# Summing one block's expert values on VectorE, and a gate matrix laid out in 8 KB runs

## The chip, the cores and the metric

One core of a Trainium2 chip runs one program. The metric is the time of one execution on the device, in microseconds; the figure for a kernel is the median of its runs. Engines are named as the profile names them: PE is TensorE's matmul, PEld its weight load, DVE is VectorE, ACT is ScalarE, POOL is GpSimd, SP is SyncE, which issues most DMAs.

## The reference, cut to what matters

A block of a transformer: a mixer (mLSTM heads beside forgetting attention), then a channel mixer that fetches experts by product keys. Only the second is touched by the change. For each of 1024 tokens it finds 128 of 16,384 experts (8 heads, 16 each), and each expert is one row of `peer_u` and one row of `peer_v`, both 1024 floats:

```
ids  = 128 experts of each token          # from two top-16 lists per head
gate = softmax over the 16 of each head
u    = u_emb[ids]
act  = gelu(einsum('ted,td->te', u, xb))
w    = gate * act
out  = h_res + einsum('te,ted->td', w, v_emb[ids])
```

All of it is float32.

## The kernel before, in words

The 1024 tokens are four segments of two blocks of 128 tokens. The middle two segments (512 tokens) are computed **densely**: every expert is applied to every token, and a gate matrix that is zero where a token did not choose an expert picks out the right terms. The first and the last segment are computed **sparsely**: the rows of the chosen experts are gathered by indirect DMAs, 512 KB each (128 rows of 4 KB).

*Sparse part.* `gather_rows` makes the items of one block. A u item gathers the r-th expert row of each of the 128 tokens (line 326), so that token and partition agree; DVE multiplies it with the tokens and sums along the row in one instruction (line 335). A v item gathers, for one token, its 128 expert rows (line 362), so that partitions are experts, and the indices are first transposed (lines 353 to 360). Four such tokens make one step of PE: eight matmuls in the program, sixteen matmul records in the trace, which contract the 128 experts with the weights (line 384) into one accumulator `po` for the whole block. The weights `wT` are laid out by `weigh` (line 338), once per block, and a DVE copy puts four columns of them into a stationary tile of zeros before each step (line 378). At the end the residual is loaded, added and stored (lines 387 to 390). `gather_items` (line 395) gives the order in a segment: all u items of the first block (A), then four v items of A and four u items of the second block (B) in turn, and last the 128 v items of B alone.

*Gate matrix.* `gates` (line 1105) builds, for 32 tokens at a time, a tile `G` of 128 x 128 x 32 (key i, key j, token; 16 KB for each partition j), two buffers of it in turn. Each is stored to the array `gd` in memory (line 1155, 2 MB, 16 times). The last-but-one stage of the program holds this, the top-k of the last segment and some u products that are spilled for later.

*Dense stage.* It begins once `gd` is complete. The 16,384 experts are 128 tiles of 128, in 32 groups of four. For a tile `dense_u` computes the 512 tokens' products (lines 290, 1172), or loads them where they were spilled (line 1169; 12 of the 32 groups, called K below; the other 20 are R); for a group `weights` loads its gates into `Gt` (line 1220, 1 MB), DVE multiplies (line 1224), ACT and DVE split the result into a high and a low half (lines 1227, 1228); `dense_v` multiplies with the values of the group (line 1246) and DVE adds what comes out to `acc` (line 1251). Every matrix that is streamed in is split into halves likewise: ACT makes the high one (line 279), DVE the low one (line 284), with two buffers of each. The groups run K K, ten R, and then K and R in turn.

*What sets the order.* The items of the last segment are spread over the dense stage by a pacer (lines 1012 to 1049): two beats follow each product of `dense_u` (24 matmuls, or none where it is loaded) and one follows each tile of values in one half of the columns (12 matmuls), 512 beats in all, and 1.08 items are asked for in each. A gather may start when the latest dense matmul at that point of the program is done (line 1031), and its item is used `LAG = 5` steps later. There are 11 buffers for gathered rows (`GATH` 7 and `GATHV` 4). So the u items of A fall on the first 6.8 groups, the items of the second quarter and third quarter on the groups up to 21.6, and the 128 v items of B on groups 21.6 to 29. After that the dense stage runs alone. Within these bounds a planner orders every engine's instructions ahead of time, from its own estimate of durations; on the chip each engine works its list in that order.

Of the kernel before, what the change touches and what calls it, by code (L numbers as in the profile page):

```python
# [9 lines left out]
F32 = mybir.dt.float32  # L10
F32R = mybir.dt.float32r
I32 = mybir.dt.int32
U32 = mybir.dt.uint32
AF = mybir.ActivationFunctionType
OP = mybir.AluOpType
# [4 lines left out]
P = 128  # L20
D = 1024
KT = 8
# [5 lines left out]
NH_M = 4  # L28
# [17 lines left out]
DENSE = (1, 2)  # L46
NB = 2
# [3 lines left out]
GRP = 4  # L51
# [29 lines left out]
GATH = 7  # L81
GATHV = 4

JV = 14

RATE = 1.08
# [5 lines left out]
def _block_kernel(ctx, tc, nc, I, out, dbg):  # L92

    def pool(name, bufs, stack=ctx, **kw):
        return stack.enter_context(tc.tile_pool(name=name, bufs=bufs, **kw))

    cp = pool("const", 1)
    big = pool("big", 1)
    wp = pool("wp", 2)
    pp = pool("peer", 2)  # L100
    dp = pool("dram", 1, space=DRAM)
# [14 lines left out]
    st = pool("state", 1, front)  # L116
# [20 lines left out]
    dve, act, pe, pool_e, sync = nc.vector, nc.scalar, nc.tensor, nc.gpsimd, nc.sync  # L137
# [4 lines left out]
    identr = cp.tile([P, P], F32R, tag="identr", name="identr")  # L142
    dve.tensor_copy(identr, tmpi)
    ident = identr.bitcast(F32)
    negidr = cp.tile([P, P], F32R, tag="negidr", name="negidr")
    dve.tensor_scalar(negidr, tmpi, -1.0, None, op0=OP.mult)
    negid = negidr.bitcast(F32)
    tmpc = cp.tile([P, P], F32, tag="tmpc", name="tmpc")

    mask_st = cp.tile([P, P], F32R, tag="mask_st", name="mask_st")  # L150
    pool_e.memset(tmpc, 0.0)
    pool_e.affine_select(out=tmpc, in_=tmpc, compare_op=OP.is_ge, fill=-BIG, base=0,
                         pattern=[[1, P]], channel_multiplier=-1)
    dve.tensor_copy(mask_st, tmpc)

    tmpc2 = cp.tile([P, P], F32, tag="tmpc", name="tmpc2")
    mask_ts = cp.tile([P, P], F32R, tag="mask_ts", name="mask_ts")
    pool_e.memset(tmpc2, 0.0)
    pool_e.affine_select(out=tmpc2, in_=tmpc2, compare_op=OP.is_ge, fill=-BIG, base=0,
                         pattern=[[-1, P]], channel_multiplier=1)  # L160
    dve.tensor_copy(mask_ts, tmpc2)
    ones = cp.tile([P, P], F32, tag="ones", name="ones")
    pool_e.memset(ones, 1.0)
    blk2 = cp.tile([P, P], F32, tag="blk2", name="blk2")
    pool_e.memset(blk2, 0.0)
    pool_e.memset(blk2[0:64, 0:64], 1.0)
    pool_e.memset(blk2[64:128, 64:128], 1.0)
    eye4 = cp.tile([NH_M, NH_M], F32, tag="eye4", name="eye4")
    dve.tensor_copy(eye4, ident[0:NH_M, 0:NH_M])
    iota_i = cp.tile([P, P], I32, tag="tmpc", name="iota_i")  # L170
    pool_e.iota(iota_i, pattern=[[1, P]], base=0, channel_multiplier=0)
# [17 lines left out]

    Zm = []  # L190
    for i in range(2):
        z = cp.tile([P, NB, 66], F32R, tag=f"Zm{i}", name=f"Zm{i}")
        zc = cp.tile([P, 66], F32, tag="tmpc", name="zc")
        pool_e.memset(zc, 0.0)
        pool_e.memset(zc[:, 64:65], -1.0)
        dve.tensor_copy(z, zc.unsqueeze(1).broadcast_to([P, NB, 66]))
        Zm.append(z)
    gmix = cp.tile([P, KT], F32, tag="gmix", name="gmix")
    sync.dma_start(gmix, I["g_mix"])
    gbias = cp.tile([72, 1], F32, tag="gbias", name="gbias")  # L200
    sync.dma_start(gbias, I["g_bias"])
    taps = cp.tile([P, 8, 4], F32, tag="taps", name="taps")
    sync.dma_start(taps, I["taps"])
    gqk = cp.tile([P, 2], F32, tag="gqk", name="gqk")
    sync.dma_start(gqk, I["g_qk"])
    gq8 = cp.tile([P, 1], F32, tag="gq8", name="gq8")
    dve.tensor_scalar(gq8, gqk[:, 0:1], 0.125, None, op0=OP.mult)
    epsc = cp.tile([P, 1], F32, tag="epsc", name="epsc")
    pool_e.memset(epsc, EPS)

    def rsqrt(o, x, scale, t):
# [101 lines left out]
    def gather_rows(S, lb, share, room):  # L313

        b = S.xb0 + lb
        G = SimpleNamespace(S=S, lb=lb, b=b)
        G.actv = pp.tile([P, P], F32, tag="actv", name="actv")
        xn = []

        def ask(r):  # L320
            if r == 0:
                x_ = pp.tile([P, D], F32, tag="xng", name="xng", bufs=1)
                sync.dma_start(x_, xnd[b * P:(b + 1) * P, :])
                xn.append(x_)
            t = room("u", lb, r).tile([P, D], F32, tag="g", name="gu")
            d = pool_e.indirect_dma_start(out=t, out_offset=None, in_=I["peer_u"],  # L326
                                          in_offset=bass.IndirectOffsetOnAxis(ap=S.idx[:, lb, r:r + 1], axis=0))
            return t, d

        def use(r, t):  # L330
            if r % 16 in share:
                pool_e.tensor_tensor(t, t, xn[0], op=OP.mult)
                return lambda: act.activation(t, t, AF.Copy, accum_out=G.actv[:, r:r + 1])
            else:
                dve.scalar_tensor_tensor(t, t, 1.0, xn[0], op0=OP.mult, op1=OP.mult, accum_out=G.actv[:, r:r + 1])  # L335
        G.u = [(lambda r=r: ask(r), lambda t, r=r: use(r, t)) for r in range(P)]

        def weigh():
            wv = pp.tile([P, P], F32, tag="wv", name="wv", bufs=1)
            gelu = act.activation(wv, G.actv, AF.Gelu)  # L340
            with tc.issue_after(gelu.ins):
                act.preload_act_table_set(EXPLN)
            dve.tensor_mul(wv, wv, S.gate[:, lb, :])
            G.po = po_pool.tile([P, 2, 512], F32, tag="po", name="po")
            pe.transpose(G.po[:, 0, 0:P], wv, ident)
            G.wT = pp.tile([P, 4, 32], F32, tag="wT", name="wT", bufs=1)
            dve.tensor_copy(G.wT, G.po[:, 0, 0:P].rearrange("p (q j) -> p q j", q=4))

        def ask_v(tok):
            if S.idT is None:  # L350

                S.idT = []
                tp = po_pool.tile([P, 2, 512], F32, tag="po", name="idt")
                for k in range(NB):
                    idf = pp.tile([P, P], F32, tag="wv", name="idf", bufs=1)
                    dve.tensor_copy(idf, S.idx[:, k, :])
                    pe.transpose(tp[:, k, 0:P], idf, ident)
                    idT = pp.tile([P, P], I32, tag="idT", name="idT")
                    dve.tensor_copy(idT, tp[:, k, 0:P])
                    S.idT.append(idT)  # L360
            t = room("v", lb, tok % 32).tile([P, D], F32, tag="g", name="gv")
            d = pool_e.indirect_dma_start(out=t, out_offset=None, in_=I["peer_v"],  # L362
                                          in_offset=bass.IndirectOffsetOnAxis(ap=S.idT[lb][:, tok:tok + 1], axis=0))
            return t, d

        rows = {}

        def use_v(j, q, t):


            rows[q] = t
            if q < 3:
                return
            if j == 0:
                weigh()

            z = Zs[j % 2]
            dve.tensor_copy(z[:, :, 31:32], G.wT[:, :, j:j + 1])
            last = None
            with tc.high_priority():  # L380
                for n in range(2):
                    for q_ in reversed(range(4)):
                        with tc.issue_after(last.ins) if last else nullcontext():
                            last = pe.matmul(G.po[32 * q_:32 * q_ + 32, n, :], z[:, q_, 31 - j:63 - j],  # L384
                                             rows[q_][:, n * 512:(n + 1) * 512], start=(j == 0), stop=(j == 31))
            if j == 31:
                h2 = room("h", lb, j).tile([P, D], F32, tag="g", name="h2o")
                sync.dma_start(h2, h2d[b * P:(b + 1) * P, :])
                dve.tensor_add(h2, h2, G.po.rearrange("p a b -> p (a b)"))
                sync.dma_start(out[b * P:(b + 1) * P, :], h2)  # L390
        G.v = [(lambda tok=32 * q + j: ask_v(tok), lambda t, j=j, q=q: use_v(j, q, t))
               for j in range(32) for q in range(4)]
        return G

    def gather_items(S, share, room):
# [663 lines left out]
    for i in range(-1, len(SEGS)):  # L1059
# [9 lines left out]
        if i >= 0:  # L1069
            S = segs[i]  # L1070
# [28 lines left out]

    nb, xb0, nx = 2 * NB, sum(SEGS[:DENSE[0]]), DX  # L1100
    TG = 32
    gd = dp.tile([nx // TG, P, P, TG], F32, tag="gd", name="gd")
    dps = pool("dps", 2, space=PSUM)

    def gates(S, gb):

        for b in range(NB):
# [22 lines left out]
            for tg in range(P // TG):  # L1130
                G = gb.tile([P, P, TG], F32, tag="G", name="G")
                for q in range(TG // 4):
# [19 lines left out]
                    with nullcontext():  # L1152
                      act.copy(G[:, :, q * 4:q * 4 + 4].rearrange("p i t -> p t i"),  # L1153
                             bk.rearrange("p (t i) -> p t i", t=4))
                sync.dma_start(gd[(NB * (S.sg - DENSE[0]) + b) * (P // TG) + tg], G)
                yield


# [26 lines left out]
    gbs.close()  # L1185
    mid.close()
    up = pool("ahead", AHEAD + 1, reuse_waits="tile")
    rows3 = [0]

    def room3(kind, lb, i):  # L1190
# [24 lines left out]
    def weights(g):  # L1215

        res = []
        Gt = ds_.tile([P, nx // TG, GRP, TG], F32, tag="Gt", name="Gt", bufs=2)
        e0 = order[g] * GRP
        sync.dma_start(Gt, gd[:, :, e0:e0 + GRP, :].rearrange("b j i t -> j b i t"))  # L1220
        for ii in range(GRP):
            w = ws[g * GRP + ii]
            w3 = w.rearrange("p (b t) -> p b t", t=TG)
            dve.tensor_mul(w3, w3, Gt[:, :, ii, :])
            Wh = ds_.tile([P, 512], F32R, tag="Wh", name="Wh", bufs=2 * GRP)
            Wl = ds_.tile([P, 512], F32R, tag="Wl", name="Wl", bufs=2 * GRP)
            act.copy(Wh, w)  # L1227
            dve.tensor_sub(Wl, w, Wh.bitcast(F32))
            res.append((Wh, Wl))
        return res  # L1230
# [80 lines left out]
```

## Time and profile before

| | us |
|---|---|
| median of 3 runs (lowest, highest) | 3333.57 (3333.47, 3339.92) |
| the profiled execution | 3322.29 |
| its span in the profile | 3320.4 |

| engine | busy us | share of the span | instructions |
|---|---|---|---|
| PE | 3004.0 | 90% | 14225 |
| DVE | 2210.0 | 67% | 5506 |
| ACT | 1060.2 | 32% | 1961 |
| POOL | 1375.3 | 41% | 1233 |

DMA moved 931.18 MB, on average 280 GB/s. The profile is read by stage: a share over the whole span mixes stages with different limits. "Busy" of several instructions that overlap counts the stretch once in the tables of windows; the mean duration of one instruction can be longer than the distance from its start to the next one's.

### The profile page before, as it was taken

What the parts mean: (1) busy time and instruction counts of PE and PEld (TensorE: products, weight loads), DVE (VectorE), ACT (ScalarE), POOL (GpSimd) and SP (SyncE); (2) the same over time, 40 slices, a digit from 0 to 9 for tenths busy, and PEclk for the clock granted to TensorE, in tenths of its full rate; (3) what the DMA queues carried; (4) which work ended last, traced back from release to release, by engine and by line L of the source; (5) the groups of instructions that cost most, each with busy time, mean ns of one, the idle gap of its engine ahead of it and who ended that gap; (6) DMA issues with size and microseconds to landing.
All of it is one profiled execution on the core that took longest, in us unless ns stands there. A gap on an engine that the chain in (4) does not pass through costs nothing. (4 is left out here: it accounts for less than half of the span.)

```text
span 3320.4 us, 41585 instructions
## 1 busy us (share of the span) xinstructions
PE 3004.0 (90%) x14225; PEld 2196.0 (66%) x14225; DVE 2210.0 (67%) x5506; ACT 1060.2 (32%) x1961; POOL 1375.3 (41%) x1233
## 2 busy tenths in 40 slices
PE   8999789567977889999999876999999999999999
PEld 4566567444754667766468765777777777776666
DVE  3242579996546996556378996888667777674443
ACT  1323423223222322222246683222322322232221
POOL 1000055575456554445564302544435444443442
PEclk9988899878979889999999888999999999999999
DMA  4535488998999988888986637988889999998995
GB/s 136 137 109 138 152 292 276 288 317 292 342 309 360 324 286 246 253 264 312 357 307 232 257 166 263 315 305 318 291 299 366 346 357 340 336 335 317 340 339 199
DMA packets 373816, 931.18 MB, mean 280 GB/s; under 512 B 57268, under 2 KB 143508, under 8 KB 371556
## 3 DMA queue, kind: packets, MB, share of 16 engines
q0 software_dynamic: 161216, 552.56, 47.4%
q1 hardware_dynamic: 212388, 375.96, 33.5%
q8 instruction: 112, 1.84, 0.2%
q14 instruction: 100, 0.82, 0.1%
HBM read 860.91 MB, written 67.47 MB: 280 GB/s over the span
## 5 line engine op out<-in xcount | busy, mean ns | idle before, releaser
L326 POOL DMA_INDIRECT gu<-in_peer_u,idx x512 | 598.5, 1169 | 749.7 <-DVE gu L335 165.9
L362 POOL DMA_INDIRECT gv<-in_peer_v,idT x512 | 547.5, 1069 | 605.0 <-PE po L384 360.7
L335 DVE SCALAR_TENSOR_TENSOR gu<-gu,xng 128x1024 f32<-128x1024 f32 x496 | 614.7, 1255 | 95.9 <-DMA gu<-in_peer_u,idx 89.2
L279 ACT CAST wh<-raw 128x1024 fp32r<-128x1024 f32 x288 | 301.9, 1049 | 822.2 <-PE vo L1246 282.3
L284 DVE TENSOR_TENSOR wl<-raw,wh 128x1024 fp32r<-128x1024 f32 x262 | 323.3, 1234 | 283.3 <-ACT wh L279 235.8
L1246 PE MATMUL vo<-wh,Wh 128*128 128x512 f32 x1024 | 377.6, 397 | 34.7 <-ACT Wh L1227 18.2
L1246 PE MATMUL vo<-wl,Wh 128*128 128x512 f32 x1024 | 403.3, 394 | 0.0
L1246 PE MATMUL vo<-wh,Wl 128*128 128x512 f32 x1024 | 401.4, 393 | 0.0
L303 PE MATMUL fp<-hnh,raw 128*128 128x256 f32 (+1 forms) x1024 | 253.8, 406 | 36.7 <-DVE frs L630 23.1
L384 PE MATMUL po<-gv,Z 128*32 128x512 f32 x2048 | 257.9, 613 | 9.5 <-DMA gv<-in_peer_v,idT 8.4
L1246 PEld LDWEIGHTS vo<-wh,Wh 128*128 128x128 f32 x1024 | 194.6, 190 | 98.6 <-issue 23.5
L303 PEld LDWEIGHTS fp<-hnh,raw 128*128 128x128 f32 x1024 | 203.9, 203 | 78.7 <-DVE frs L630 24.7
L290 PE MATMUL du<-xh,wl 128*128 128x512 f32 x640 | 250.3, 391 | 0.0
L290 PE MATMUL du<-xl,wh 128*128 128x512 f32 x640 | 250.2, 391 | 0.0
L290 PE MATMUL du<-xh,wh 128*128 128x512 f32 x640 | 249.9, 390 | 0.0
L1246 PEld LDWEIGHTS vo<-wl,Wh 128*128 128x128 f32 x1024 | 194.1, 190 | 48.9 <-issue 8.4
L1246 PEld LDWEIGHTS vo<-wh,Wl 128*128 128x128 f32 x1024 | 193.9, 189 | 48.2 <-issue 7.5
L430 PE MATMUL tk<-raw,hnh 128*128 128x512 f32 (+1 forms) x416 | 195.3, 617 | 4.1 <-DMA raw<-in_wt 3.0
L1151 PE MATMUL gout<-A,B 128*128 128x128 f32 x1024 | 155.8, 303 | 43.2 <-DVE A L1149 16.8
L1251 DVE TENSOR_TENSOR acc<-acc,vo 128x512 f32<-128x512 f32 x256 | 167.2, 684 | 32.6 <-PE vo L1246 30.2
L1151 PEld LDWEIGHTS gout<-A,B 128*128 128x128 f32 x1024 | 141.1, 209 | 66.3 <-ACT G L1153 23.4
L1227 ACT CAST Wh<-w 128x512 fp32r<-128x512 f32 x128 | 79.4, 621 | 289.0 <-PE vo L1246 164.4
(407 smaller groups left out, 5165.4 us busy)
## 6 DMA issues: line engine op xcount, KB each, us to landing
raw<-in_ut SPq DMA_DIRECT2D x128, 512.0 KB
raw<-in_peer_v SPq DMA_DIRECT2D x128, 512.0 KB
raw<-in_wf SPq DMA_DIRECT2D x64, 512.0 KB
gd<-G SPq DMA_DIRECT2D x16, 2048.0 KB
Gt<-gd SPq DMA_DIRECT2D x32, 1024.0 KB
raw<-in_wt SPq DMA_DIRECT2D x48, 512.0 KB
raw<-in_wq SPq DMA_DIRECT2D x48, 512.0 KB
raw<-in_wo SPq DMA_DIRECT2D x32, 512.0 KB
```

Of the source, the lines that this page charges most:

```text
L279: seen["act"] = act.copy(h, raw)
L284: seen["dve"] = dve.tensor_sub(l, raw, h.bitcast(F32))
L290: seen["pe"] = pe.matmul(o, w, x[:, c], start=(first and i == 0), stop=(last and i == 2))
L303: pe.matmul(o, raw[:, k * P:(k + 1) * P], xh[:, k, c], start=(k == 0), stop=(k == KT - 1))
L326: d = pool_e.indirect_dma_start(out=t, out_offset=None, in_=I["peer_u"], in_offset=bass.IndirectOffsetOnAxis(ap=S.idx[:, lb, r:r + 1], axi ...
L335: dve.scalar_tensor_tensor(t, t, 1.0, xn[0], op0=OP.mult, op1=OP.mult, accum_out=G.actv[:, r:r + 1])
L362: d = pool_e.indirect_dma_start(out=t, out_offset=None, in_=I["peer_v"], in_offset=bass.IndirectOffsetOnAxis(ap=S.idT[lb][:, tok:tok + 1], ...
L384: last = pe.matmul(G.po[32 * q_:32 * q_ + 32, n, :], z[:, q_, 31 - j:63 - j], rows[q_][:, n * 512:(n + 1) * 512], start=(j == 0), stop=(j ...
L430: pe.matmul(b[0:w, :], xh[:, k, s0:s0 + w], raw[:, k % 2 * 512:(k % 2 + 1) * 512], start=(k == 0), stop=(k == KT - 1))
L1151: pe.matmul(bk[:, u * P:(u + 1) * P], B[:, u, :], A[:, u, :], start=True, stop=True)
L1246: seen["pe"] = pe.matmul(bks[b], w[:, cw], v, start=(ii == 0 and i == 0), stop=(ii == GRP - 1 and i == 2))
L1251: dve.tensor_add(o, o, bks[b])
```

## The change

The v items of the second block of the last segment (`VDVE`) are done as its u items are: item r gathers the r-th expert row of each of the 128 tokens, by `S.idx` itself, and DVE multiplies it with the token's weight and adds it to a sum `G.sum` of 128 x 1024 floats. Before the first of them ACT computes gelu, DVE multiplies with the gate, and the sum is loaded with the residual from `h2d`; after the last the sum is stored. The 512 matmul records of that block, its weight transpose, its 32 column copies, the final addition, one index transpose and one reload of an ACT table are no longer there.

The array `gd` is laid out as [group of four tiles][j][32-token block][4 tiles x 32 tokens] in place of [32-token block][j][i][token]. A load of `Gt` then reads 8 KB in one run for each partition, where it read 16 runs of 512 B; a store of `G` writes 32 runs of 512 B for each partition, 1 MB apart, where it wrote one of 16 KB.

Constant tiles that only the first stages use are placed in the pool `st`, whose memory is given back when these stages end. The sum tile takes 4 KB for each partition.

```diff
+VDVE = ((3, 1),)
...
-    ones = cp.tile([P, P], F32, tag="ones", name="ones")
+    ones = st.tile([P, P], F32, tag="ones", name="ones")
...
-                for k in range(NB):
+                for k in [k for k in range(NB) if (S.sg, k) not in VDVE]:
...
-        G.v = [(lambda tok=32 * q + j: ask_v(tok), lambda t, j=j, q=q: use_v(j, q, t))
-               for j in range(32) for q in range(4)]
+        def ask_r(r):
+            t = room("v", lb, r).tile([P, D], F32, tag="g", name="gr")
+            d = pool_e.indirect_dma_start(out=t, out_offset=None, in_=I["peer_v"],
+                                          in_offset=bass.IndirectOffsetOnAxis(ap=S.idx[:, lb, r:r + 1], axis=0))
+            return t, d
+
+        def use_r(r, t):
+
+            if r == 0:
+                G.wv = pp.tile([P, P], F32, tag="wr", name="wr", bufs=1)
+                gelu = act.activation(G.wv, G.actv, AF.Gelu)
+                dve.tensor_mul(G.wv, G.wv, S.gate[:, lb, :])
+                G.sum = sums.tile([P, D], F32, tag="gsum", name="gsum", bufs=1)
+                sync.dma_start(G.sum, h2d[b * P:(b + 1) * P, :])
+            dve.scalar_tensor_tensor(G.sum, t, G.wv[:, r:r + 1], G.sum, op0=OP.mult, op1=OP.add)
+            if r == P - 1:
+                sync.dma_start(out[b * P:(b + 1) * P, :], G.sum)
+        if (S.sg, lb) in VDVE:
+            G.v = [(lambda r=r: ask_r(r), lambda t, r=r: use_r(r, t)) for r in range(P)]
+        else:
+            G.v = [(lambda tok=32 * q + j: ask_v(tok), lambda t, j=j, q=q: use_v(j, q, t))
+                   for j in range(32) for q in range(4)]
...
-    gd = dp.tile([nx // TG, P, P, TG], F32, tag="gd", name="gd")
+    gd = dp.tile([P // GRP, P, nx // TG, GRP * TG], F32, tag="gd", name="gd")
...
-                sync.dma_start(gd[(NB * (S.sg - DENSE[0]) + b) * (P // TG) + tg], G)
+                sync.dma_start(gd[:, :, (NB * (S.sg - DENSE[0]) + b) * (P // TG) + tg, :].rearrange("g j c -> j g c"),
+                               G.rearrange("p (g i) t -> p g (i t)", i=GRP))
...
+    sums = pool("sums", 1, reuse_waits="tile")
...
-        e0 = order[g] * GRP
-        sync.dma_start(Gt, gd[:, :, e0:e0 + GRP, :].rearrange("b j i t -> j b i t"))
+        sync.dma_start(Gt, gd[order[g]].rearrange("j b (i t) -> j b i t", i=GRP))
```

## Rows read from the trace of the kernel before

**Rows 1.** Windows by stage: busy us by engine, granted PE clock, DMA share, GB/s.

```profile
core 0: us, PE busy (x) PEld busy (x) DVE busy (x) ACT busy (x) POOL busy (x), PEclk, DMA share, GB/s
1671.00:1925.00 254.00, 226.93 (x1306) 185.79 (x1302) 229.19 (x809) 151.42 (x278) 122.05 (x110) 0.92 0.71 264
1925.00:2007.40 82.40, 61.23 (x387) 52.30 (x387) 70.24 (x198) 76.95 (x145) 0.00 (x0) 0.94 0.35 150
2007.40:2024.20 16.80, 0.00 (x0) 0.00 (x0) 1.34 (x3) 0.61 (x1) 0.00 (x0) 0.53 1.00 353
2133.50:2319.80 186.30, 176.85 (x769) 145.06 (x769) 156.86 (x235) 51.04 (x64) 88.31 (x70) 0.99 0.89 310
2319.80:2992.00 672.20, 671.72 (x3164) 510.49 (x3165) 469.71 (x695) 195.57 (x252) 301.74 (x267) 1.00 0.93 334
2992.00:3290.00 298.00, 298.00 (x1527) 200.87 (x1526) 126.36 (x183) 75.14 (x97) 122.38 (x118) 1.00 0.89 319
3290.00:3320.40 30.40, 24.16 (x107) 19.68 (x105) 12.15 (x16) 3.15 (x3) 0.00 (x0) 0.98 0.22 87
```

**Rows 2.** Chain that ended last, 3010 to 3043 us: start, us, what.

```profile
3010.19 7.48 PE vo L1246 x32
...
3024.35 11.15 PE vo L1246 x48
3035.49 1.85 PE po L384 x16
3037.35 5.69 PE du L290 x24
```

**Rows 3.** Groups by line, 2992 to 3290 us: busy us, mean ns | idle before.

```profile
L384 PE MATMUL po<-gv,Z 128*32 128x512 f32 x512 | 62.6, 598 | 0.0
L284 DVE TENSOR_TENSOR wl<-raw,wh 128x1024 fp32r<-128x1024 f32 x43 | 52.7, 1226 | 79.8 <-ACT wh L279 50.9 <-issue 14.3 <-PE du L290 13.8
L1251 DVE TENSOR_TENSOR acc<-acc,vo 128x512 f32<-128x512 f32 x52 | 34.5, 685 | 12.6 <-PE vo L1246 11.3 <-issue 1.1
L1228 DVE TENSOR_TENSOR Wl<-w,Wh 128x512 fp32r<-128x512 f32 x27 | 18.6, 691 | 29.2 <-ACT Wh L1227 19.3 <-PE vo L1246 5.8 <-issue 4.1
L1224 DVE TENSOR_TENSOR w<-w,Gt 128x512 f32<-128x512 f32 x27 | 18.0, 685 | 2.7 <-ACT w L1173 2.7
```

**Rows 4.** Groups by line, 2133.5 to 2319.8 us, four R groups with u items.

```profile
L335 DVE SCALAR_TENSOR_TENSOR gu<-gu,xng 128x1024 f32<-128x1024 f32 x69 | 82.1, 1221 | 2.1 <-DMA gu<-in_peer_u,idx 2.1
L1246 PE MATMUL vo<-wh,Wh 128*128 128x512 f32 x129 | 45.9, 402 | 11.2 <-DVE acc L1251 11.2
L284 DVE TENSOR_TENSOR wl<-raw,wh 128x1024 fp32r<-128x1024 f32 x32 | 39.2, 1225 | 20.9 <-ACT wh L279 20.9
```

**Rows 5.** Timeline of DVE, 2117.5 to 2135 us: start us, us, instruction.

```profile
2117.51 1.22 DVE L335 SCALAR_TENSOR_TENSOR gu<-gu,xng 128x1024 f32<-128x1024 f32 x1
2118.66 0.08 DVE L335 DVE_READ_ACCUMULATOR gu<-gu,xng 128x1 f32 x1
2118.66 1.22 DVE L335 SCALAR_TENSOR_TENSOR gu<-gu,xng 128x1024 f32<-128x1024 f32 x1
...
2132.71 2.48 DVE L1251 TENSOR_TENSOR acc<-acc,vo 128x512 f32<-128x512 f32 x4
```

**Rows 6.** Chain that ended last, 2003 to 2134 us: start, us, what.

```profile
2003.93 0.92 ACT G L1153
...
2005.56 0.60 ACT G L1153
...
2007.36 7.26 DMA gd<-G
...
2014.70 8.14 DMA Gt<-gd
...
2122.75 8.79 DMA gu<-in_peer_u,idx
```

**Rows 7.** Windows with little but one transfer: a store of gd, loads of Gt.

```profile
1940.00:1950.00 10.00, 7.38 (x52) 6.23 (x51) 9.22 (x28) 9.80 (x20) 0.00 (x0) 1.00 0.50 211
2018.80:2024.80 6.00, 0.54 (x1) 0.50 (x2) 1.94 (x4) 1.18 (x3) 0.00 (x0) 0.50 1.13 345
```

More of the change, by code (lines that the diff above doesn't have):

```diff
@@ L144, in _block_kernel @@
     ident = identr.bitcast(F32)
-    negidr = cp.tile([P, P], F32R, tag="negidr", name="negidr")
+    negidr = st.tile([P, P], F32R, tag="negidr", name="negidr")
     dve.tensor_scalar(negidr, tmpi, -1.0, None, op0=OP.mult)
@@ L148, in _block_kernel @@
     tmpc = cp.tile([P, P], F32, tag="tmpc", name="tmpc")
-    mask_st = cp.tile([P, P], F32R, tag="mask_st", name="mask_st")
+    mask_st = st.tile([P, P], F32R, tag="mask_st", name="mask_st")
     pool_e.memset(tmpc, 0.0)
@@ L156, in _block_kernel @@
     tmpc2 = cp.tile([P, P], F32, tag="tmpc", name="tmpc2")
-    mask_ts = cp.tile([P, P], F32R, tag="mask_ts", name="mask_ts")
+    mask_ts = st.tile([P, P], F32R, tag="mask_ts", name="mask_ts")
     pool_e.memset(tmpc2, 0.0)
@@ L161, in _block_kernel @@
     dve.tensor_copy(mask_ts, tmpc2)
-    ones = cp.tile([P, P], F32, tag="ones", name="ones")
+    ones = st.tile([P, P], F32, tag="ones", name="ones")
     pool_e.memset(ones, 1.0)
-    blk2 = cp.tile([P, P], F32, tag="blk2", name="blk2")
+    blk2 = st.tile([P, P], F32, tag="blk2", name="blk2")
     pool_e.memset(blk2, 0.0)
@@ L167, in _block_kernel @@
     pool_e.memset(blk2[64:128, 64:128], 1.0)
-    eye4 = cp.tile([NH_M, NH_M], F32, tag="eye4", name="eye4")
+    eye4 = st.tile([NH_M, NH_M], F32, tag="eye4", name="eye4")
     dve.tensor_copy(eye4, ident[0:NH_M, 0:NH_M])
@@ L191, in _block_kernel @@
     for i in range(2):
-        z = cp.tile([P, NB, 66], F32R, tag=f"Zm{i}", name=f"Zm{i}")
+        z = st.tile([P, NB, 66], F32R, tag=f"Zm{i}", name=f"Zm{i}")
         zc = cp.tile([P, 66], F32, tag="tmpc", name="zc")
@@ L197, in _block_kernel @@
         Zm.append(z)
-    gmix = cp.tile([P, KT], F32, tag="gmix", name="gmix")
+    gmix = st.tile([P, KT], F32, tag="gmix", name="gmix")
     sync.dma_start(gmix, I["g_mix"])
-    gbias = cp.tile([72, 1], F32, tag="gbias", name="gbias")
+    gbias = st.tile([72, 1], F32, tag="gbias", name="gbias")
     sync.dma_start(gbias, I["g_bias"])
-    taps = cp.tile([P, 8, 4], F32, tag="taps", name="taps")
+    taps = st.tile([P, 8, 4], F32, tag="taps", name="taps")
     sync.dma_start(taps, I["taps"])
-    gqk = cp.tile([P, 2], F32, tag="gqk", name="gqk")
+    gqk = st.tile([P, 2], F32, tag="gqk", name="gqk")
     sync.dma_start(gqk, I["g_qk"])
-    gq8 = cp.tile([P, 1], F32, tag="gq8", name="gq8")
+    gq8 = st.tile([P, 1], F32, tag="gq8", name="gq8")
     dve.tensor_scalar(gq8, gqk[:, 0:1], 0.125, None, op0=OP.mult)
-    epsc = cp.tile([P, 1], F32, tag="epsc", name="epsc")
+    epsc = st.tile([P, 1], F32, tag="epsc", name="epsc")
     pool_e.memset(epsc, EPS)
```

## The prediction

> **What bounds the kernel now.** I read the table of windows by stage first [rows 1], then the chain of waits, then the groups by line inside two stages. Both edits act after 1671 us. The store of the gate matrix lies in 1671 to 2007; its loads, the gathers and the dense matmuls lie behind it.
>
> The v items of block B run from 2992 to 3290. There PE is busy for all of the 298 us at a granted clock of 1.00 (the 2.4 GHz level), DVE for 126.36, DMA at a share of 0.89 [rows 1]. The chain through this stage is PE alone: pieces of vo and du with a step of po between them [rows 2]. So this stage is bound by PE, with DMA close behind and DVE far from it. The stage of A's v items and B's u items (2319.8 to 2992) is bound by PE too: 671.72 of 672.20 us. The stretch of R groups that carries A's u items is the one place where DVE already takes a row for each item as it will in block B: PE is busy for 176.85 of 186.3 us, DVE for 156.86, DMA at 0.89 [rows 1].
>
> **The v items of block B: what goes.** One step of po is 1.85 us in the chain [rows 2], and 512 records in steps of 16 [rows 3] are 32 steps: 32 x 1.85 = 59.2 us of PE. What PE keeps in these 298 us is 1014 dense matmuls: 663 vo records (three groups of 221 to the stage) and 351 du records, which is the 1527 of the stage [rows 1] less 512 and one transpose. Their distance is 11.15 / 48 = 0.232 to 7.48 / 32 = 0.234 us by the chain [rows 2], so 235 to 237 us. If nothing else bound, the stage would be 298 - 59 = 239 us.
>
> **What comes.** 128 DVE instructions over 128 x 1024 floats with two tensor inputs. The trace has no multiply by a column and add; the nearest row is the u item, with the same shape and the same number of tensor inputs: 1.221 us mean [rows 4], and 1.145 us from start to start where they follow each other (2117.51 to 2118.66) [rows 5]. I take the latter, since a DVE that is always behind runs them back to back: 128 x 1.145 = 146.6 us. The other end is 128 x 1.221 = 156.3. DVE keeps 43 halvings, 52 additions to acc and 54 small ones [rows 3]; at start-to-start distances (1.14 us; 2.48 / 4 = 0.62; the same 0.62) that is 49.0 + 32.2 + 33.5 = 114.7 us, at full durations 52.7 + 34.5 + 18.6 + 18.0 = 123.8. So DVE needs **261 to 280 us**, more than PE's 239: the bound of this stage passes from PE to DVE.
>
> DMA moves the same rows (128 gathers of 512 KB, in another order). It needed 0.89 x 298 = 265 us of all its engines [rows 1]; about seven loads of Gt fall in the stage and each gets cheaper by some 0.6 us (below), so 261. Two resources need 261 us out of 298, and PE 239.
>
> How near to such a floor does a stage come? The R stretch has 769 dense matmuls x 0.232 = 178 us of PE work in 186.3 us, and DVE work of 69 x 1.145 + 32 x 1.14 + 65 x 0.62 = 156 us, 83% [rows 1, 4]. Its visible loss is one sort: PE waits 11.2 us for additions to acc [rows 4], and those stand in DVE's list behind an item whose gather is late: a gather issued at 2122.75 lands 8.79 us later [rows 6], then come one u item and four additions [rows 5], then PE. That is 5% over the largest need where the others have room. In block B two needs tie at 261 and DVE's list is nearly full, so I take 10%: 261 x 1.10 = **287 us, 11 us less than 298**. The ends: 266 (2% over the floor, a gain of 32) and 313 (20% over, a loss of 15).
>
> **The start of block B.** Item 0 waits for the sum, a DMA that the code issues only when that item is used. Behind it in DVE's list stand the other items and the halvings for PE, and all 11 gather buffers stay taken. The planner can move work ahead of it. Price: 0 to 8.8 us, the time that a loaded DMA takes under load [rows 6]; I take 3. The gelu, the gate multiplication and the loads were there before (the transposes and 32 column copies go). The final addition and the store change nothing: the dense stage ends 30 us later [rows 1], and that tail has no items.
>
> **The gate matrix.** A load of Gt now reads 128 runs of 8 KB. Loads of 512 B runs alone go at 345 GB/s, with the DMA engines fully taken [rows 7]: 1.05 MB in 3.0 us. A store with 16 KB runs moves 211 GB/s x 10 us = 2.1 MB in 0.50 x 10 us [rows 7], 5.0 us, 422 GB/s; at that rate a load is 2.5 us. So 0.5 to 0.6 us for each of 32 loads, off a stage that PE bounds, except that a gather queued beside one lands a little sooner in the R stretch: I take -2 us, between 0 and the whole 11.2 us that PE waits for acc there [rows 4].
>
> A store now has runs of 512 B. The trace has none; the nearest row is the loads of such runs: 2.1 MB at 345 GB/s is 6.1 us instead of 5.0. Inside 1671 to 1925 DMA has 29% free and SP prefetches four tiles ahead, which hides 1 us. From 1925 to 2007 one G tile takes eight times (2005.56 - 2003.93 =) 1.63 us = 13.0 us of ACT [rows 6], and two buffers hide any store under that. The last store is bare: it takes 7.26 us, then the first Gt 8.14 us, with PE idle from 2007 to 2024 [rows 1, 6]. There the edit costs +1.1 and gives back 0.6: I take +1. Upper end: if a run of 512 B costs twice as much to store, 12.2 us for a store, 14.5 with the 2.3 us beyond transfer time that the last one shows: +7 on the last store and 1.5 us over the 13.0 for each of some six tiles, so +16.
>
> The trace weighs against one rule here. The loads before step 2 MB from run to run and still move 345 GB/s [rows 7]. The Trainium skill ("DMA: Bandwidth & Descriptors", section "Latency and other measured facts") gives copies whose rows lie a large power of two apart a lower rate, 164 GB/s at 2 MiB against 207 at 512 KiB. By it the stores, now 1 MB apart, would be the slow end just named, an estimate of some 20 to 25% loss on top of the 1.1 us. The loads, which carry the same pattern, do not show it.
>
> **Sum.** Against the profiled execution of 3322.3 us (span 3320.4): -11 + 3 - 2 + 1 = -9, so 3313. The median of the runs, 3333.6, is 11 above that execution; I carry the difference over: **3324.5 us**. The constants' move and the missing index transpose are worth nothing: POOL and ACT have room there.
>
> **Rivals.**
> *DVE's list starves PE (slower).* If a late gather stops DVE in block B as it does in the R stretch, every halving behind it is late, PE stops, and because a gather waits for a dense matmul, the next gathers are late too. For it: in a K group 17.3 items x 1.145 = 19.8 us of DVE meet only 22 us of vo, beside 4 halvings, 8 additions and 8 small ones (14.5 us): 34 against 22, nothing to lend. Against it: R groups alternate with K. Also against it: `dense_u` runs five tiles ahead, so three products of the next R group fall into a K group. It decides from 298 / 261 = 1.14 times the floor; at 1.20 it is +15, with the other three terms +17: 3351.
> *Nothing measurable.* DMA is the limit and stays at the share of 0.89 that it has in both stages with the same mix [rows 1]: 261 / 0.89 = 293, a gain of 5, and -5 + 3 - 2 + 1 = -3: 3331. Against it: 0.93 in the stage between.
> *At the floor.* The planner spreads items so well that DVE hardly waits: 266 us, and the R stretch gets half its 11 us back: 3333.6 - 32 - 5 = 3297.
> *The layout costs what block B gives:* the slow stores, +16 in place of +1, and -11 + 3 - 2 + 16 = +6: 3340. For it: no store of such runs is in the trace; against it: the loads of such runs, 2 MB apart, are fast.
>
> **How the numbers follow.** The forecast has 0.40, the floor 0.14, nothing measurable 0.20, starving DVE 0.20, slow stores 0.06. A measurement of this kernel tells some 0.2% (6.7 us) from no change. The forecast's own range, 3317 to 3332, reaches into that band with a tenth of its weight. Faster: 0.36 + 0.14 + 0.02 = 0.52; same: 0.04 + 0.17 + 0.02 = 0.23; slower: the rest, 0.25. The range for 8 in 10 goes from just above the floor case to the price of a starving DVE: 3300 to 3349.
>
> **What would show it.** Right: in block B no po, 128 DVE items of 1.15 to 1.25 us, DVE busy for over 90% of it, PE for 80 to 88%, the stage 280 to 295 us from the last u item to the last v item; stores of gd within 6 to 7 us and PE starting by 2026. Wrong: DVE idle in block B behind gathers (starving), DMA above 0.93 with DVE below 88% (DMA the bound), PE's clock below 1.00 there (its gaps then cost twice), ACT waiting on G after 1925 (slow stores), or a stage before 1671 that has moved.

## The result

The changed kernel takes 3297.21 us (median of 4 runs, 3285.65 to 3300.83), against 3333.52 for the kernel before: ratio 0.9888, 95% interval 0.9853 to 0.9923. In a later set of runs it was 3288.22 against 3321.89: ratio 0.9908 [0.9885, 0.9930]. So it is faster by 1%, some 31 to 37 us, where 9 were forecast. The direction was right, the size wrong by a factor of three to four, and the time lies just under the stated range. Between the two profiled executions the gain is only 24 us: 37.6 less in the last stage, 2.4 more at the last store of the gate matrix, 11.5 more in the middle stretch, from the first gate multiplication to the last u item.

The windows of the profile after, with the same columns as [rows 1], cut at events: the end of the last G tile, the four R groups, the first gate multiplication, the last u item, the end of the program.

```profile
2007.30:2026.50 19.20, 0.00 (x0) 0.00 (x0) 1.22 (x3) 0.49 (x1) 0.00 (x0) 0.56 0.95 325
2138.60:2333.30 194.70, 182.48 (x769) 149.24 (x770) 157.63 (x236) 51.03 (x64) 86.66 (x70) 0.96 0.83 297
2025.30:2999.10 973.80, 950.27 (x4334) 737.28 (x4335) 714.10 (x1060) 278.05 (x358) 431.43 (x372) 0.98 0.88 321
2999.10:3296.70 297.60, 269.67 (x1148) 218.92 (x1147) 286.23 (x302) 78.50 (x102) 158.82 (x122) 0.95 0.90 335
```

The last row is the stage that the DVE edit makes, from the last u item to the end of the program: 297.60 us, DVE busy for 286.23 (96%), PE for 269.67 (91%). In the kernel before the same two events are 335.2 us apart (2985.2, the last u item, to 3320.4). A second profile of the kernel before shows both stretches again (its first row is cut 1.4 us behind the first gate multiplication):

```profile
2012.60:2974.00 961.40, 945.17 (x4334) 734.16 (x4335) 712.38 (x1058) 277.57 (x357) 435.04 (x372) 0.99 0.91 325
2974.00:3309.10 335.10, 328.94 (x1662) 226.15 (x1660) 145.31 (x208) 81.25 (x104) 127.12 (x122) 0.99 0.83 300
```

So the stage goes from 335.1 to 297.6 us, by 37.5, and the bound passes from PE (328.94 of 335.10) to DVE. The groups by line in that stage of the kernel after, to be held against [rows 3] (which leave out the last 30 us). Line numbers have moved: L286 and L1274 are L284 and L1251 of the kernel before, and L407 is the new item. The last row is the kernel before, over its whole 335 us:

```profile
L407 DVE SCALAR_TENSOR_TENSOR gsum<-gr,wr,gsum 128x1024 f32<-128x1024 f32 x128 | 164.0, 1281 | 1.3
L286 DVE TENSOR_TENSOR wl<-raw,wh 128x1024 fp32r<-128x1024 f32 x47 | 57.2, 1217 | 2.3 <-ACT wh L281 1.8 <-issue 0.4
L1274 DVE TENSOR_TENSOR acc<-acc,vo 128x512 f32<-128x512 f32 x68 | 43.9, 678 | 1.1 <-PE vo L1269 1.1
L395 POOL DMA_INDIRECT gr<-in_peer_v,idx x122 | 159.4, 1307 | 116.0 <-DVE gsum L407 59.3 <-issue 27.8 <-DVE acc L1274 13.8
L284 DVE TENSOR_TENSOR wl<-raw,wh 128x1024 fp32r<-128x1024 f32 x47 | 57.7, 1228 | 84.8 <-ACT wh L279 55.9 <-issue 14.3 <-PE du L290 13.8
```

The third number, idle before, is what to read: DVE waited 84.8 us before its 47 halvings in the kernel before and waits 2.3 before the same 47 now. It has no time to wait; POOL waits for it instead, 59.3 us for a buffer that an item still holds.

### The profile page after: what moved, and what is told of

The parts are those of the page before. It is cut to its first block, busy times and chain, and to the rows that moved or that the text cites. A ratio compares the mean times of both kernels' runs of the same rounds, so it can differ in the third digit from the quotient of the medians.

```text
span 3296.7 us, 40747 instructions
## 1 busy us (share of the span) xinstructions
PE 2952.3 (90%) x13711; PEld 2191.7 (66%) x13711; DVE 2355.0 (71%) x5598; ACT 1057.5 (32%) x1959; POOL 1409.4 (43%) x1233
## 2 busy tenths in 40 slices
DMA packets 375860, 931.11 MB, mean 282 GB/s; under 512 B 57268, under 2 KB 143508, under 8 KB 371556
## 4 chain that ended last, share of the span: by engine, by line
PE 59%; DVE 18%; DMA 10%; issue 7%; ACT 4%; POOL 3%; another core or an unknown queue 0%; SPq 0%; POOLq 0%; DVEq 0%; ACTq 0%
PE vo L1269 16%; PE du L292 9%; PE fp L292 6%; DVE gu L337 6%; PE tk L452 6%; PE po L386 5%; PE fp L305 4%; DMA gu<-in_peer_u,idx 4%; DMA gv<-in_peer_v,idT 2%; PE gout L1173 2%; POOL gu L328 2%; PE q L292 2%; PE pv L806 2%; PE q L305 1%; PE fs L793 1%
## 5 line engine op out<-in xcount | busy, mean ns | idle before, releaser
L364 POOL DMA_INDIRECT gv<-in_peer_v,idT x384 | 412.2, 1073 | 437.4 <-PE po L386 217.7
L286 DVE TENSOR_TENSOR wl<-raw,wh 128x1024 fp32r<-128x1024 f32 x262 | 322.6, 1231 | 205.0 <-ACT wh L281 178.0
L395 POOL DMA_INDIRECT gr<-in_peer_v,idx x128 | 166.1, 1297 | 125.7 <-DVE gsum L407 59.3
L386 PE MATMUL po<-gv,Z 128*32 128x512 f32 x1536 | 195.9, 620 | 9.1 <-DMA gv<-in_peer_v,idT 9.0
L1274 DVE TENSOR_TENSOR acc<-acc,vo 128x512 f32<-128x512 f32 x256 | 165.9, 681 | 15.8 <-PE vo L1269 13.6
```

Source lines behind the costliest of these rows:

```text
L286: seen["dve"] = dve.tensor_sub(l, raw, h.bitcast(F32))
```

## The experiments

Times of a stage are from one profile each; ratios are against the kernel before, run beside them.

**e1: the DVE edit with the old layout** (the moved constants stay).

```diff
-    gd = dp.tile([P // GRP, P, nx // TG, GRP * TG], F32, tag="gd", name="gd")
+    gd = dp.tile([nx // TG, P, P, TG], F32, tag="gd", name="gd")
...
-        sync.dma_start(Gt, gd[order[g]].rearrange("j b (i t) -> j b i t", i=GRP))
+        sync.dma_start(Gt, gd[:, :, order[g] * GRP:(order[g] + 1) * GRP, :].rearrange("b j i t -> j b i t"))
```

> The changed kernel with the gate matrix laid out as before (stores of 16 KB runs, loads of 512 B runs); block B's values stay on DVE. Every engine's list is that of the changed kernel, only these DMAs differ. Theory: the DVE edit alone is worth some 37 us (from A's last u item, 2985 in the kernel before, to the end: 335 us before, 298 after) and the layout takes back 14 of them (2.4 us at the last store, the rest where A's u items run). Then the span is about 3283 us, ratio to before 0.985 to 0.989, and A's u stretch of four R groups is back at 186 us from 195. Rival: the longer stretches in the changed kernel's profile are chance or come from memory being placed otherwise; then the span is about 3297, ratio 0.989 to 0.993.

```profile
3011.10:3308.80 297.70, 269.85 (x1149) 219.10 (x1147) 286.23 (x302) 78.72 (x102) 159.05 (x122) 0.95 0.92 335
```

Ratio 0.9912 [0.9891, 0.9933]. From the last u item to the end: 297.7 us. But the stretch before it stays long, 975.4 us, with the old layout and every engine's list that of the changed kernel. The longer middle stretch of the first profile (973.8 against 962.3) does not need the new layout, and the theory that the layout takes back 14 us falls.

**e2: the layout alone,** with the moved constants (`VDVE = ()`).

> The kernel before with the new layout of the gate matrix and the moved constants; no block is summed on DVE. Theory: the layout costs 14 us, span about 3334 against 3320, ratio 1.002 to 1.006; the last store takes 9.7 us in place of 7.3, four R groups with u items take 195 us in place of 186. Rival: layout is worth nothing or a little (the prediction's -1): ratio 0.998 to 1.001, four R groups at 186.

```profile
3000.60:3336.20 335.60, 329.24 (x1662) 226.16 (x1660) 144.81 (x208) 81.17 (x104) 127.19 (x122) 0.99 0.82 299
```

Ratio 1.0023 [1.0009, 1.0038]: the layout with the moved memory costs, about 8 us (3 to 13). The last stage is untouched, 335.6 us. From the issue of the last store to that of the first load it is 9.6 us, against 7.3; the middle stretch is 975.9.

**e5 and e6: both kernels once more.** The changed kernel as it is, and the kernel before with the same instructions in the same order.

> The changed kernel once more, to see how far a single profile carries. From A's last u item to the end: 298 us again (theory: VectorE sets it, so it hardly varies; the four profiles so far have 297.4 to 298.3). The stretch from the first gate multiplication to A's and B's last u item: 974 in its first profile, 962 in the kernel before, 969 to 985 in four others; if that is chance, another value in 960 to 985. Ratio to before 0.989 to 0.994.

> The kernel before, with the same instructions in the same order (only line numbers differ). If its 962 us from the first gate multiplication to the last u item were chance, it now shows 965 to 985; if what was added in all the other kernels (constants in another pool, the sum's memory) costs some 10 us there, it shows 958 to 966 again. From the last u item to the end 335 us in either case.

Changed kernel: ratio 0.9908 [0.9885, 0.9930]; middle stretch 962.4 us this time, last stage 297.0. Kernel before: 962.8 (its first gate multiplication starts at 2011.2, the last u item at 2974.0) and 335.1. So the middle stretch moves by 11 us between two executions of one and the same changed program, while the last stage repeats within 1 us. A single profile carries the last stage; it doesn't carry the middle one.

```profile
2020.60:2983.00 962.40, 943.27 (x4334) 732.58 (x4335) 713.54 (x1060) 278.04 (x358) 435.39 (x372) 0.99 0.89 325
2983.00:3280.00 297.00, 269.44 (x1149) 218.80 (x1147) 286.32 (x302) 78.54 (x102) 158.36 (x122) 0.95 0.89 336
```

**e7: the moved memory alone** (old layout, `VDVE = ()`, the sum's pool left in).

> The kernel before with nothing but the moved constants and the pool for the sum (old layout, no block summed on VectorE). Every engine's list is that of the kernel before. Theory: memory placement is worth nothing, ratio 0.998 to 1.002, and the 1.0023 of the run with the new layout comes from the layout alone. Rival: placement itself costs the 8 us, ratio 1.001 to 1.004.

Ratio 1.0012 [0.9997, 1.0027], which lies in the ranges of both the theory and the rival; middle stretch 969.8, last stage 335.6. What of e2's 8 us is layout and what is placement stays open; the profile accounts for some 2 us of layout, at the last store. That the moved memory costs something in the middle stretch isn't excluded: both profiles of the kernel before have 962 to 963 us there, and of the ten profiles with the moved constants (e8 and e12 apart, which change that stretch) nine have 969 to 985 and only e5 has 962.

**e3: loads in 512 B runs on the chip's side.**

```diff
-        Gt = ds_.tile([P, nx // TG, GRP, TG], F32, tag="Gt", name="Gt", bufs=2)
+        Gt = ds_.tile([P, nx // TG, GRP * TG + 4], F32, tag="Gt", name="Gt", bufs=2)[:, :, 0:GRP * TG].rearrange("p b (i t) -> p b i t", i=GRP)
```

> The changed kernel, with a gap of 16 B in the loaded tile after each 512 B, so that a load's runs are 512 B on the chip's side though 8 KB in memory. Stores as in the changed kernel. Theory: each DMA engine takes the queues' packets in turn, so a load in packets of 8 KB takes the larger share from the gathers (4 KB) that run beside it, and one in packets of 512 B the smaller; the u item that a DVE addition stands behind then lands earlier. With 512 B packets the four R groups come back to 186 to 188 us and the span to some 3286 to 3289. Rivals: the stretch is longer for another reason that the load's packet size does not touch (195 us stays), or the packets go by the memory side's runs (then the packet count in the profile does not change and nothing is told).

Nothing is told: the page counts 375,860 packets, exactly as for the changed kernel, so the gap on the chip's side did not cut the packets. Ratio 0.9937 [0.9915, 0.9959], middle stretch 984.6, last stage 297.4.

**e4: the store's runs off the power of two.**

```diff
-    gd = dp.tile([P // GRP, P, nx // TG, GRP * TG], F32, tag="gd", name="gd")
+    gd = dp.tile([P // GRP, P + 1, nx // TG, GRP * TG], F32, tag="gd", name="gd")[:, 0:P]
```

> The changed kernel with one unused row of 8 KB more in each group of the gate matrix: a store's runs of 512 B then lie 1 MB + 8 KB apart in place of 1 MB. Theory: the store's 9.7 us come from the number of its packets (4096 in place of 128), not from where they fall: the last store stays at 9 to 10 us, ratio as the changed kernel's. Rival: the distance of a power of two slows it: the last store falls to 7.3 to 8.5 us and G is never waited for.

The last store takes 9.41 us, beside 9.71 and 9.45 in the two profiles of the changed kernel and 7.26 and 7.27 in those of the kernel before. The distance is worth 0.0 to 0.3 us of the 2.3. By the rule of the Trainium skill that the prediction cited ("DMA: Bandwidth & Descriptors", section "Latency and other measured facts") the store would have lost an estimated 20 to 25% to the distance, 1.2 to 1.5 us of the 6.1 that the prediction works out for its transfer; this trace does not show it for runs of 512 B, 1 MB apart. That section of the Trainium skill gives its rates for another case: copies from memory to memory in rows of 16 KiB, each partition's row at the pitch named. Here the partitions lie 8 KB apart, and one partition's own runs 1 MB. Ratio 0.9933 [0.9910, 0.9956], middle stretch 969.5, last stage 298.3. The chain of waits of this run:

```profile
2017.15 9.41 DMA gd<-G
2026.65 7.96 DMA Gt<-gd
```

**e9: more work on DVE in block B.**

```diff
             dve.scalar_tensor_tensor(G.sum, t, G.wv[:, r:r + 1], G.sum, op0=OP.mult, op1=OP.add)
+            if r % 2:
+                dve.tensor_add(t[:, 0:512], t[:, 0:512], t[:, 512:1024])
```

> The changed kernel; behind every second item of block B VectorE adds the two halves of the row it has just used (128 x 512, the result is never read): 64 x 0.60 = 38 us more on DVE, nothing more for PE and DMA. From A's last u item to the end the changed kernel takes 297 to 298 us in five profiles, DVE busy for 286. Theory (DVE's list sets this stage): 335 us. Rival (PE with 270, or DMA at a share of 0.90, sets it and DVE has some slack): 300 to 318.

334.4 us from the last u item to the end, 36.8 more than 297.6 for 39.8 us of DVE work (326.03 against 286.23). Of what DVE got more, nine tenths come back in the time: DVE's list sets the stage.

```profile
2986.30:3320.70 334.40, 264.22 (x1149) 215.51 (x1147) 326.03 (x366) 79.07 (x102) 169.94 (x122) 0.91 0.83 299
```

**e10: less work on DVE in block B.** Each item covers 512 of the 1024 columns; the other 512 are left out of the sum.

> The changed kernel with half of each item: only the first 512 columns of block B's values are summed, the others are left out. 128 x 0.60 = 77 us less on DVE, gathers unchanged. Theory (DVE's list sets the stage, PE's 1148 dense matmuls come next with 260 to 266 us): 266 to 275 us from A's last u item to the end, in place of 298. Rival (DMA at 0.90 sets it): 285 to 298.

```profile
2986.20:3036.00 49.80, 48.08 (x213) 39.47 (x211) 41.32 (x60) 16.78 (x25) 30.90 (x25) 1.00 1.03 404
3036.00:3086.00 50.00, 47.54 (x194) 38.63 (x195) 37.82 (x50) 12.69 (x17) 26.90 (x24) 0.93 0.95 365
3086.00:3136.00 50.00, 45.97 (x194) 36.92 (x192) 38.79 (x55) 14.77 (x19) 26.31 (x22) 0.97 0.99 377
...
2986.20:3275.10 288.90, 269.35 (x1149) 219.49 (x1147) 221.95 (x302) 78.04 (x102) 141.46 (x122) 0.97 0.91 345
```

288.9 us: with 64 us less of DVE work (221.95 against 286.23) the stage loses only 8.7. The rival's number is met: the next bound stands 9 us below. DMA is at 0.95 to 1.03 in the first 150 us, PE is busy for 269 of the 289; the run doesn't tell the two apart.

**e11: items asked for earlier.**

```diff
-        count[0] += n * RATE
+        count[0] += n * (1.3 if asked[0] >= 3 * P else RATE)
...
+        asked[0] += k
```

> The changed kernel, with 1.3 items asked for in a beat from the first v item of block B on, in place of 1.08: the 128 items then fall on 98 beats, and 70 in place of 50 or so are left without any. Theory (block B ended near DVE's need because its late items run into the stretch behind the last gather, which the prediction counted as free of items): DVE has more than it can do in the 98 beats (6.2 groups x 42 us = 260), and PE has two to four groups left when the items are done (65 us and more), so 310 to 325 us from A's last u item to the end. Rival (the items run at DVE's need wherever they are asked for, and the rest goes beside them): 295 to 303.

296.8 us; the last item starts at 3295.1, 5 us before the end, as in the changed kernel (3291.6). The number is the rival's, but the run decides nothing between the two: every engine's list in its trace, DVE's 5598 instructions and POOL's 1233 among them, is in the order of the changed kernel, and the gathers of block B start as early against the last u item (the first 16.8 us before it, 16.9 there). Asking for the items earlier left the planner's order as it was, so the run is a third execution of the same lists (297.6, 297.0 and 296.8 us for the last stage; 973.8, 962.4 and 977.0 for the middle stretch). Whether another order of the items would cost time is not tested.

**e8: both blocks of the last segment on DVE** (old layout, `VDVE = ((3, 0), (3, 1))`).

> Block A of the last segment is summed on VectorE too, old layout. In the stage of A's v and B's u items PE has 665 us of work, 59 of it po, and DVE 463; DVE would take 128 x 1.2 = 154 more, less 7 for the copies: 610, PE 606. Theory (the stage takes the larger need plus some 4%, as block B's did): 635 us, 30 less than now; ratio 0.979 to 0.985. Rival: two engines tied at the same need wait for each other and the stage stays at 655 to 670: ratio 0.988 to 0.993.

```profile
2328.70:2940.00 611.30, 577.12 (x2444) 466.79 (x2443) 574.41 (x741) 176.25 (x229) 348.19 (x266) 0.97 0.97 351
2940.00:3273.30 333.30, 297.02 (x1296) 243.48 (x1294) 305.71 (x327) 91.49 (x118) 153.80 (x119) 0.95 0.89 315
```

Ratio 0.9883 [0.9862, 0.9904], median 3281.5. The first of the two stages loses more than expected (611.3, 656.1 in e1), but PE's dense work of that time is only put off: 1296 matmuls are left at the last u item where e1 has 1149, and the last stage takes 333.3 us where e1 has 297.7. Together 944.6 against 953.8. It is the fastest median of the runs that do the whole work, but its interval overlaps that of the changed kernel run beside it (e5).

**e12: e8, with every fourth low half of a value tile made by GpSimd.**

```diff
-                    v2 = halves(I["peer_v"][e0:e0 + 2 * P, cv].rearrange("(i p) c -> p i c", p=P), tiles=2)
+                    v2 = halves(I["peer_v"][e0:e0 + 2 * P, cv].rearrange("(i p) c -> p i c", p=P), 4, tiles=2)
```

> Both blocks of the last segment on VectorE, old layout, and every fourth low half of a value tile in the dense stage made by GpSimd. In the run with both blocks VectorE has some 890 us of work in the 944 from A's first v item to the end; some 30 halves of 1.15 us leave it (35 us), and GpSimd takes 2.4 us for each, beside gathers that take 1.2 to 1.3. Theory (DVE sets these stages too): 20 to 30 us less than with both blocks alone, ratio 0.979 to 0.984. Rival: the halves come later from GpSimd and hold up the gathers behind them: ratio 0.986 to 0.995.

Ratio 0.9974 [0.9959, 0.9990]: most of the gain is gone, more than the rival had. A half takes GpSimd 2.5 us and the gathers are queued behind it in its list; that the loss comes from there is argued, not tested.

## Why the prediction was wrong, point by point

**The bound passes from PE to DVE: right.** No po in block B, DVE busy for 96% (over 90% forecast), PE for 91% (80 to 88%). e9 shows that DVE sets the stage.

**"261 x 1.10 = 287 us, 11 us less than 298", and behind it 30 us, since "the dense stage ends 30 us later ... and that tail has no items": this step failed.** The need of DVE was set against the 298 us between the first v item and the last step of po, and the 30.4 us behind [rows 1] were added unchanged. That border is one that the order of PE's work made. In the changed kernel the items run on beside the dense work to its end: DVE's last four instructions are items, the last starting at 3291.6, 5 us before the end. Almost all of the gain lies behind the old border:

| us | before | forecast | after |
|---|---|---|---|
| last u item to the first v item | 6.8 | 6.8 + 3 | 3.1 |
| block B's v items | 298.0 | 287 | 290.7 |
| behind the last of them | 30.4 | 30.4 | 3.8 |

The two windows of the kernel after, and what DVE's timeline ends with:

```profile
3002.20:3292.90 290.70, 266.57 (x1135) 216.36 (x1133) 283.14 (x296) 78.00 (x100) 156.03 (x121) 0.96 0.90 338
3292.90:3296.70 3.80, 0.00 (x0) 0.00 (x0) 0.00 (x0) 0.00 (x0) 0.00 (x0) 0.50 0.34 138
3287.66 5.24 DVE L407 SCALAR_TENSOR_TENSOR gsum<-gr,wr,gsum 128x1024 f32<-128x1024 f32 x4
```

That 287 comes so near to 290.7 is luck: DVE's work in that stretch is 283 us, the tail's with it, not 261, and it loses 3%, not 10%. Once DVE sets the pace, its whole remaining list has to be held against the whole remaining 335 us. The sum that should have been made: DVE's 145 us of those 335 (second profile of the kernel before), less 7 for the copies and the final addition, plus the items. With the prediction's own two prices, 146.6 and 156.3, that is 285 and 294; measured 286. Four per cent over it is 297.6. That DVE's list is the bound rests on e9 and e10; that the items must reach to the end in any order is not shown, since e11 did not change the order.

**The item's price: too low.** 1.145 us from start to start was taken from the u item; the range's other end was 1.221. The sum's item takes 1.32 where the next item follows it (36 times), and 1.20 where something else does (91 times):

```profile
3107.67 1.27 DVE L407 SCALAR_TENSOR_TENSOR gsum<-gr,wr,gsum 128x1024 f32<-128x1024 f32 x1
3108.87 1.21 DVE L286 TENSOR_TENSOR wl<-raw,wh 128x1024 fp32r<-128x1024 f32 x1
3110.01 3.91 DVE L407 SCALAR_TENSOR_TENSOR gsum<-gr,wr,gsum 128x1024 f32<-128x1024 f32 x3
```

From 3107.67 to 3108.87 is 1.20; from 3110.01 three items take 3.91, the last of them 1.27. At full durations all 128 take 164.0 us, 8 over the upper end; from start to start 36 x 1.32 + 92 x 1.20 = 158 us, 11 over the 146.6 of the sum. This error alone would have made the gain smaller; what is left of DVE's 286 us for the halvings and additions, 128, is 10 less than the 138 in the kernel before, where they ran with gaps between them, and covers most of it.

**The 10% for lost time: too much.** DVE loses 4%. The R stretch, from which the loss was drawn, is one where PE waits for DVE [rows 4]; where DVE sets the pace, PE's and DMA's slack of 9 us (e10) seems enough to keep it fed.

**The start of block B, +3: nothing.** The planner put the load of the sum at 1924.85, a thousand microseconds ahead of its use.

**The layout, -1: not borne out.** The last store takes 9.7 us, +2.4, where +1.1 was priced (9.4 to 9.8 in the eight profiles with the new layout, 7.3 with the old one). The first Gt lands after 8.21 us, where it did after 8.14. Over all profiles the 0.6 does come back: 7.6 to 8.2 us with the new layout (seven profiles, 7.8 on average, e3 left out), 8.1 to 9.0 with the old one (five, 8.6). The gate build from 1925 to the last tile still takes 82.3 us, so G is not waited for:

```profile
1925.00:2007.30 82.30, 59.51 (x386) 50.48 (x386) 70.39 (x198) 76.80 (x146) 0.00 (x0) 0.96 0.56 160
```

DMA's share there is 0.56, where it was 0.35 [rows 1]: the stores cost more, beside other work. The R stretch's -2 can't be seen: 194.7 us in one profile against 186.3, but the middle stretch of the same program varies by 11 and more. By e2 the layout with the moved memory costs 0.1 to 0.4%, so the gain comes from the DVE edit alone.

**The signs.** One of the signs of being wrong came: PE's clock is 0.95 in the last stage. Stores within 6 to 7 us and items of 1.15 to 1.25 us did not (9.7; 1.28 on average), and PE starts at 2026.7.

**The rivals.** "At the floor" named 3297, which is the measured time, but by luck: of its two prices, 266 us for the stage of 298 and half of the 11 us in the R stretch, neither came (290.7, and no gain seen in the R stretch). Starving DVE did not happen: DVE idles 11 us of 298. The slow stores cost a third of their upper end (2.4 us of 7) at the one place where they are bare, and the distance of 1 MB was not their cause.

## What to carry to other kernels

When an edit moves work from the engine that sets the end to another, compare each engine's whole remaining list with the whole remaining time, not with the window that the old bound had cut out: slack behind that window is slack for the new bound too. Before reading a difference of ten microseconds in a stage where transfers and three engines are close to one another, look at a second profile of the same program. Before reading an experiment that is to move work in time, compare the engines' lists: e11 left them all as they were. And a transposed layout moves the short runs, it does not remove them; ask which end is bare.

## What was not expected of the hardware

- A DVE instruction that adds to its own output takes 1.32 us from start to start when the next one adds to the same tile, 1.20 when another instruction follows; a u item of the same size, followed by a u item on another tile, 1.145 [rows 5]. That the shared tile is the reason is not tested.
- A 2 MB store in runs of 512 B lands after 9.4 to 9.8 us, whether the runs lie 1 MB or 1 MB + 8 KB apart; one in runs of 16 KB after 7.3.
- PE's granted clock is 0.95 in the last stage, 1.00 in the kernel before [rows 1], though PE is busy for 91% of it. It is at the lower of the two levels from 3051 to 3057, 3126 to 3132 and 3201 to 3207 us, each time behind short waits of PE, 2 to 3 us together, and again after PE's last matmul. In the three stretches 32 matmuls take some 0.63 us each, where 0.39 is usual. Over the whole stage the dense matmuls are no dearer: 187.8 us of vo and 83.7 of du, 186.5 and 86.2 in the kernel before.
- A gather's issue takes POOL 1.307 us on average beside the items; beside po it took 1.04 (122.38 us for 118 gathers, [rows 1]). The busier DVE is, the longer it takes: 1.16 in e10 (DVE busy for 77% of the stage), 1.31 here (96%), 1.40 in e9 (97%). Why is not tested.
